# Adaptive modulation by matmuls, q and k projected by tokens, filter norms taken first

## The chip, the cores and the metric

The kernel runs on one core of a Trainium2 chip. The metric is the device time of one execution in microseconds, as the median of several runs. A core has five engines that run at the same time, each through its own list of instructions in order: TensorE (PE; matmuls, results go to PSUM; its weight loads are listed as PEld), VectorE (DVE), ScalarE (ACT), GpSimd (POOL) and SyncE (SP), which here issues nearly all DMAs. They wait for each other by semaphores.

## The reference

One layer of a diffusion backbone, for 2048 image tokens ("latent", cond vector `c`) and 256 text tokens ("prompt", cond vector `c_ctx`), width 1024:

```python
shift1, scale1, gate1, shift2, scale2, gate2 = split(silu(cond) @ w_mod + b_mod, 6)
u = (rms_norm(x, norm1_g) * (1 + scale1) + shift1) @ w_in
u_pool, u_hy, u_q, u_k, u_v = split(u)                  # 256, 768, 512, 512, 512 columns
y_hy = hyena_mixer(u_hy, ...)                           # two gated long convolutions by FFT
q = rms_norm(u_q.reshape(B, L, 8, 64), q_norm_g)        # per head of 64 channels
k = rms_norm(u_k.reshape(B, L, 8, 64), k_norm_g)
y = concatenate([pool_mixer(u_pool), y_hy, attend(q, k, u_v)]) @ w_out
x = x + gate1 * y
x = x + gate2 * (square(relu((rms_norm(x) * (1 + scale2) + shift2) @ w_up)) @ w_down)
```

The convolution filters are made in the kernel as well. `h` is a small network over positions, and for each of two directions and two orders

```python
k = (h @ f3_w).reshape(L, 2, 2, 256) * decay            # "taps"
filters = k / (sum(abs(k), over positions) + 1e-6)      # the filter's norm, one for a channel
```

## The kernel before

All data are float32. Precise products are made of three matmuls in a shorter format (`mm3`, lines 130 to 133): both operands are split into a high and a low half, and high x high, high x low and low x high are summed. A weight tile of 512 KB is loaded by `wtile` (line 123): the high half is made by ScalarE (line 117) or GpSimd (line 119), the low half `wl` by VectorE (line 120). There are three buffers for the raw tile and three for the halves. Other products (filters, modulation, transposes) are plain float32 matmuls, each of which the trace shows as two records.

Three generators issue the work, and `weave` (line 177) takes the next step from the one that lags most behind its share of declared costs: `dense` (line 1122), `latent_mixers` (line 999) and `prompt_mixers` (line 800). A planner then orders the instructions of each engine, with the order of issue as priority. `wait_for` holds a generator until a name is in `done`.

`dense` first computes shift1 and scale1 (`modulation_first`, line 221), then `u` in five runs of up to 512 tokens (line 1135; the fourth run is the prompt's 256 tokens), eight tiles of channels each. After each tile it takes `MODU[i]` steps of `modulation_rest` (line 326), which computes the other four sixths of the modulation: one load of 256 KB and the products for one block of 128 input channels a step, VectorE for one cond vector and ScalarE with GpSimd for the other. The partial sums `macc` have channels along the free dimension and are summed over partitions by matmuls with a column of ones (line 346).

Then `proj_qkv` (line 258) projects q, k and v, in runs of 512 tokens (and one of 256), in the order of `JOBS` (line 256). For q and k a tile of 128 channels (two heads) by all tokens of the run is made with the weight as stationary operand (matmuls of 512 columns). v is made by tokens: the tokens are the stationary operand and 256 channels the moving one; it holds two weight tiles, each of half of the input channels, until the job's end. The head norms of q and k need a sum over 64 channels, that is over partitions: the squares are split, and two matmuls with the block matrix `headsum` (line 265) spread the sums to all partitions. `rstd` (line 135) makes the inverse root by four steps of ScalarE and two of VectorE. This is done for a tile in `finish`, one job later.

`filters` (line 432) runs in the latent generator while `dense` makes `u`. For each order `o` (`filter_latent`, line 477) a first loop makes the 16 taps tiles (`filter_taps`, line 398: four matmuls of 64 rows by 256 columns, a product with the loaded decay, magnitudes by ScalarE, sums of them by GpSimd) and keeps all in 16 buffers; `filter_rinv` makes the inverse norms; a second loop scales each tile (`filter_finish`, GpSimd) and transforms it (`time_to_freq`). For `o = 1` the generator waits for `u` and `ln` between the two loops. The prompt's filters (`prompt_filters`) use the same functions.

`aux_tile` (line 217) gives the one PSUM bank that the dense stream uses besides its three accumulators. After `proj_qkv` come the output projections and the MLP, with the latent attention beside them.

Of the kernel before, what the change touches and what calls it, by code (L numbers as in the profile page):

```python
# [10 lines left out]
F32 = mybir.dt.float32  # L11
# [8 lines left out]
P = 128  # L20
# [7 lines left out]
DH = 64  # L28
# [27 lines left out]
def tile_hybrid_step(ctx: ExitStack, tc: tile.TileContext, a: dict):  # L56
# [33 lines left out]
    headsum = ctile([P, P], "headsum", F32R)  # L90
    for e in range(2):
        for f in range(2):
            nc.gpsimd.memset(headsum[64 * e:64 * e + 64, 64 * f:64 * f + 64].bitcast(F32), float(e == f))

# [40 lines left out]
    def rstd(pool, ss, n, shape):  # L135

        r = pool.tile(shape, F32, tag="rsr", name="r", bufs=1)
        v = xp.tile(shape, F32, tag="tmp", name="v")
        t = xp.tile(shape, F32, tag="tmp", name="t")
# [80 lines left out]

    def modulation_first(lp):
# [18 lines left out]
        pmt = acc_tile()  # L240
        mrow = xp.tile([P, 512], F32, tag="raw", name="mrow", bufs=3)
        nc.vector.tensor_copy(mrow, pm)
        for q in range(4):
            nc.tensor.transpose(pmt[:, q * P:(q + 1) * P], mrow[:, q * P:(q + 1) * P], ident)
        pmv = pmt.rearrange("p (q j r) -> p j q r", q=4, j=4)

        def halves(t):
            return t.rearrange("p (j q) -> p j q", j=2)

# [6 lines left out]
    JOBS = ((1, 0), (1, 1), (1, 2), (1, 3), (2, 0), (0, 0), (0, 1), (0, 2), (0, 3), (2, 1))  # L256

    def proj_qkv(qp, hT, T0, n):
# [3 lines left out]
        def finish(comp, j, raw, sq):  # L262
            pss = aux_tile()[:, :n]
            for i in range(2):
                nc.tensor.matmul(pss, headsum, sq[i], start=(i == 0), stop=(i == 1))
            r = rstd(qp, pss, DH, [P, n])
            nc.vector.scalar_tensor_tensor(out=raw, in0=raw, scalar=(qg8, pvs("kg"))[comp], in1=r, op0=ALU.mult, op1=ALU.mult)
            nc.sync.dma_start(out=(qT, kT)[comp][j][:, T0:T0 + n], in_=raw)
            if comp == 1 and T0 == NL:
                nc.sync.dma_start(out=a["new_kT"][j * P:(j + 1) * P, :], in_=raw)  # L270

        def rows(dst, r0, cs):
            return dst[r0:r0 + 2 * P, cs].rearrange("(e p) c -> p e c", p=P)

        for comp, part in JOBS:
            if comp == 2:
                W = [wtile("w_v", 2 * part + kk, 4, (None, nc.gpsimd)[kk]) for kk in range(2)]
                cs = slice(part * 256, (part + 1) * 256)
                for t in range(0, n, 2 * P):
                    pp = acc_tile()  # L280
                    for e in range(2):
                        ts = slice(t + e * P, t + (e + 1) * P)
                        for k in range(KD):
                            mm3(pp[:, e * 256:(e + 1) * 256], hT[k][0][:, ts], hT[k][1][:, ts], W[k // 4][0][:, k % 4, :], W[k // 4][1][:, k % 4, :], k == 0, k == KD - 1, skip_group_check=True)
                        yield 2600
                        while todo:
                            finish(*todo.pop(0))
                    v = qp.tile([P, 2, 256], F32, tag="q", name="v")
                    nc.scalar.activation(v.rearrange("p e c -> p (e c)"), pp, AF.Copy)
                    if T0 < NL:  # L290
                        nc.sync.dma_start(out=rows(vd, T0 + t, cs), in_=v)
                    else:
                        nc.sync.dma_start(out=rows(vpd, 0, cs), in_=v)
                        nc.sync.dma_start(out=rows(a["new_v"], 0, cs), in_=v)
                continue
# [4 lines left out]
            while todo:  # L300
                finish(*todo.pop(0))
# [1118 lines left out]
```

## Time and profile before

| | |
|---|---|
| median of 3 runs | 3247.18 us (3244.32 to 3251.28) |
| the profiled execution | 3239.31 us |
| its span (first to last instruction) | 3237.4 us |
| PE busy | 3008.9 us (93%) |
| DVE busy | 2104.9 us (65%) |
| ACT busy | 1507.1 us (47%) |
| POOL busy | 1179.4 us (36%) |
| mean granted TensorE clock | 0.959 |

The profile is of one execution. Shares over the whole span hide the stages, so the views are read by stretch. In the view by windows a row is one stretch: its bounds and length, then for PE, PEld, DVE, ACT and POOL the busy microseconds with the number of instructions, then the granted clock of TensorE as a share of 2.4 GHz, the busy share of the DMA engines and the GB/s that they moved. In the groups of instructions a row names the line, the engine, the operation, the tiles (out<-in), their shapes and the count; then the busy microseconds and the mean nanoseconds of one, and after the second bar the idle time of the engine just before them and what ended it. Matmuls are pipelined: a record is longer than the distance to the next start.

### The profile page before, as it was taken

Reading aid. Unit: us, or ns where it says so; the run is one execution under the profiler, and the core shown is the slowest. Engines: PE = TensorE matmul, PEld = TensorE weight load, DVE = VectorE, ACT = ScalarE, POOL = GpSimd, SP = SyncE. Lnnn points to the kernel's source line nnn. Section 1 sums busy time; section 2 is a strip of 40 time slices with the busy share of each in tenths; the row PEclk is TensorE's granted clock in tenths of the full one; section 3 lists DMA queues with packets and bytes.
Section 4 is the critical chain, followed back from the end, with each engine's and each line's share of the span. In section 5 each row is a group of like instructions: output and inputs, shape, how many; then the busy total and the mean of one; then the engine's idle time right before and its main releaser. Section 6 shows DMA issues by size and latency. Waiting matters only on the chain.

```text
span 3237.4 us, 44877 instructions
## 1 busy us (share of the span) xinstructions
PE 3008.9 (93%) x15997; PEld 2483.3 (77%) x15997; DVE 2104.9 (65%) x3090; ACT 1507.1 (47%) x2803; POOL 1179.4 (36%) x996
## 2 busy tenths in 40 slices
PE   4989888878898899999999999899999999999999
PEld 1777677766777898986887777688878888788887
DVE  8797967997857977787666555544463444644443
ACT  3556455554656656666555554322342223432222
POOL 3777745566424523445333332311131111311111
PEclk8999888888998999999999999999999999999999
DMA  6657476556855596553334324322324223232322
GB/s 220 190 161 250 140 231 218 188 189 195 274 173 190 163 313 196 180 186 107 123 114 126 111 94 154 115 96 98 124 85 150 98 93 122 91 118 97 98 98 85
DMA packets 252862, 489.99 MB, mean 151 GB/s; under 512 B 23508, under 2 KB 124569, under 8 KB 252316
## 3 DMA queue, kind: packets, MB, share of 16 engines
q1 hardware_dynamic: 245437, 464.83, 44.1%
q0 software_dynamic: 7200, 22.28, 2.4%
q8 instruction: 127, 2.08, 0.3%
q14 instruction: 98, 0.79, 0.1%
HBM read 417.67 MB, written 70.13 MB: 151 GB/s over the span
## 4 chain that ended last, share of the span: by engine, by line
PE 68%; DVE 15%; DMA 6%; issue 4%; POOL 4%; ACT 3%; SPq 1%; DVEq 0%; ACTq 0%; POOLq 0%
PE pm L131 19%; PE pm L132 19%; PE pm L133 19%; PE po L867 3%; PE ppt L846 2%; DVE wl L120 2%; PE ps L832 1%; PE ps L833 1%; DMA dc<-in_decay 1%; POOL kk L419 1%; DVE macc L338 1%; DMA wm<-in_w_mod 1%; DVE hl L171 1%; PE pf L131 1%; POOL ssq L155 1%
## 5 line engine op out<-in xcount | busy, mean ns | idle before, releaser
L131 PE MATMUL pm<-hh,wh 128*128 128x512 f32 (+1 forms) x2240 | 850.0, 382 | 37.8 <-ACT hh L117 17.6
L120 DVE TENSOR_TENSOR wl<-wraw,wh 128x1024 fp32r<-128x1024 f32 x460 | 608.0, 1323 | 424.7 <-ACT wh L117 403.6
L132 PE MATMUL pm<-hl,wh 128*128 128x512 f32 (+1 forms) x2240 | 847.6, 379 | 16.7 <-DVE hl L171 12.4
L133 PE MATMUL pm<-hh,wl 128*128 128x512 f32 (+1 forms) x2240 | 845.1, 378 | 6.7 <-DVE wl L120 6.7
L117 ACT ACTIVATE wh<-wraw 128x1024 fp32r<-128x1024 f32 x430 | 454.5, 1058 | 765.7 <-PE pm L132 673.5
L120 POOL TENSOR_TENSOR al<-r,ah 128x512 fp32r<-128x512 f32 (+1 forms) x160 | 200.8, 1256 | 975.2 <-ACT ah L117 975.0
L131 PEld LDWEIGHTS pm<-hh,wh 128*128 128x128 f32 x2240 | 435.0, 195 | 116.8 <-ACT hh L117 19.1
L132 PEld LDWEIGHTS pm<-hl,wh 128*128 128x128 f32 x2240 | 434.6, 194 | 95.8 <-DVE hl L171 14.8
L133 PEld LDWEIGHTS pm<-hh,wl 128*128 128x128 f32 x2240 | 433.8, 194 | 81.9 <-DVE wl L120 8.0
L133 PE MATMUL pm<-ah,wl 128*128 128x512 f32 (+1 forms) x1280 | 475.8, 372 | 0.1
L131 PE MATMUL pm<-ah,wh 128*128 128x512 f32 (+1 forms) x1280 | 471.9, 372 | 4.0 <-ACT ah L117 2.5
L132 PE MATMUL pm<-al,wh 128*128 128x512 f32 (+1 forms) x1280 | 474.1, 371 | 1.2 <-POOL al L120 1.2
L1094 DVE SCALAR_TENSOR_TENSOR x<-pm,gate,x 128x512 f32<-128x512 f32 (+1 forms) x320 | 221.1, 695 | 273.3 <-PE pm L133 272.5
L131 PEld LDWEIGHTS pm<-ah,wh 128*128 128x128 f32 x1280 | 240.4, 188 | 47.0 <-ACT ah L117 2.7
L132 PEld LDWEIGHTS pm<-al,wh 128*128 128x128 f32 x1280 | 241.4, 189 | 43.7 <-POOL al L120 1.4
L133 PEld LDWEIGHTS pm<-ah,wl 128*128 128x128 f32 x1280 | 241.4, 189 | 41.8 <-issue 0.8
L838 POOL TENSOR_SCALAR sS<-sS,rl 128x736 f32<-128x736 f32 (+5 forms) x128 | 117.7, 920 | 201.1 <-DVE rl L837 127.2
L969 POOL TENSOR_TENSOR Tt<-bias,mask 128x360 f32<-128x360 f32 (+5 forms) x96 | 102.4, 1067 | 180.1 <-DVE m L981 147.5
L117 ACT ACTIVATE ah<-r 128x512 fp32r<-128x512 f32 (+1 forms) x160 | 93.8, 588 | 151.4 <-DVE r L1077 150.9
L155 POOL TENSOR_TENSOR ssq<-ssq,sqr 128x512 f32<-128x512 f32 (+1 forms) x70 | 97.7, 1396 | 135.5 <-ACT sqr L154 135.5
L986 ACT ACTIVATE sS<-sS,m 128x480 f32<-128x480 f32 (+5 forms) x128 | 77.2, 603 | 112.0 <-DVE m L985 107.7
L1077 DVE TENSOR_TENSOR r<-r 128x512 f32<-128x512 f32 (+1 forms) x160 | 118.1, 739 | 1.5 <-ACT r L1076 1.3
(317 smaller groups left out, 5044.7 us busy)
## 6 DMA issues: line engine op xcount, KB each, us to landing
wraw<-in_w_up SPq DMA_DIRECT2D x160, 512.0 KB
wraw<-in_w_down SPq DMA_DIRECT2D x160, 512.0 KB
wraw<-in_w_u SPq DMA_DIRECT2D x40, 512.0 KB
dftw<-in_S POOLq DMA_DIRECT2D x40, 512.0 KB, 6.4
wraw<-in_w_qk SPq DMA_DIRECT2D x40, 512.0 KB
wraw<-in_w_out SPq DMA_DIRECT2D x40, 512.0 KB
x<-in_xT_sample SPq DMA_DIRECT2D x64, 256.0 KB
wm<-in_w_mod SPq DMA_DIRECT2D x64, 256.0 KB
```

The source lines that it names most:

```text
L117: nc.scalar.activation(hi, raw, AF.Copy)
L120: lo_eng.tensor_tensor(out=lo, in0=raw, in1=hi.bitcast(F32), op=ALU.subtract)
L131: nc.tensor.matmul(out, lh, rh, start=start, stop=False, **kw)
L132: nc.tensor.matmul(out, lh, rl, start=False, stop=False, **kw)
L133: nc.tensor.matmul(out, ll, rh, start=False, stop=stop, **kw)
L155: nc.gpsimd.tensor_tensor(out=acc, in0=acc, in1=sq, op=ALU.add)
L838: nc.gpsimd.tensor_scalar(out=sc_[:, :tot], in0=sc_[:, :tot], scalar1=r, scalar2=1.0, op0=ALU.mult, op1=ALU.mult)
L867: nc.tensor.matmul(po[64 * e:64 * e + 64, ocol:ocol + P], vap(e, n), pt[:n, col * P:(col + 1) * P], start=(q == 0), stop=(q == len(chunks) ...
L969: nc.gpsimd.tensor_tensor(out=t_, in0=bias[e][:, bro:bro + nr, bco:bco + ncol], in1=mask[rc * 3 + cc_], op=ALU.add)
L986: nc.scalar.activation(sS[:, :n], sS[:, :n], AF.Exp, bias=m4[:, 2:3], accum_out=m4[:, 3:4])
L1077: nc.vector.tensor_tensor(out=r, in0=r, in1=r, op=ALU.mult)
L1094: nc.vector.scalar_tensor_tensor(out=xs[j], in0=po, scalar=gate2[:, j, c:c + 1], in1=xs[j], op0=ALU.mult, op1=ALU.add)
```

## The change

There are four parts. `modulation_rest` now multiplies on TensorE: a step loads four tiles of 256 KB, runs one matmul for each with the two cond vectors (padded to 32 columns) as stationary operand, into four 32-row strips of one auxiliary PSUM bank, and adds that bank to `acc`. Two halves of eight steps make all four sixths; the result is turned by four transposes (`modulation_rows`, cut out of `modulation_first`). Steps are taken after every other tile of `u`.

q and k are projected by tokens like v, in six jobs in place of ten, from weights that are stored by 256 channels (`w_qkv`). The squares are summed by heads along the free dimension, the inverse root is made on 16 columns at most, and the result is turned back to channels by transposes.

The latent filters' norms are made ahead of both orders, from taps with channels as rows (`decayT` is the decay turned). The inverse norms are spread by matmuls and scale the last weight, `f3n`, so the taps come out normed and each is transformed as it is made. Taps and transforms share one loop, which for `o = 1` stands behind the wait for `u`.

`rstd` takes a `size` for the small tiles. The `headsum` constant goes.

```diff
-    JOBS = ((1, 0), (1, 1), (1, 2), (1, 3), (2, 0), (0, 0), (0, 1), (0, 2), (0, 3), (2, 1))
+    JOBS = ((1, 0), (1, 1), (2, 0), (0, 0), (0, 1), (2, 1))
...
+        def finish(comp, part, t, raw, r, out):
+            heads = raw.rearrange("p (e h d) -> p (e h) d", e=2, h=4)
+            nc.vector.tensor_tensor(out=heads, in0=heads, in1=r[:, t // 32:t // 32 + 8, None].to_broadcast([P, 8, DH]), op=ALU.mult)
+            tr = aux_tile()
+            for c in range(2):
+                for e in range(2):
+                    nc.tensor.transpose(tr[:, (2 * c + e) * P:(2 * c + e + 1) * P], raw[:, e * 256 + c * P:e * 256 + (c + 1) * P], ident)
+            nc.scalar.activation(out[:, :, t:t + 256], tr.rearrange("p (c t) -> p c t", c=2), AF.Copy, scale=(qg8, pvs("kg"))[comp])
...
         for comp, part in JOBS:
...
+            W = [wtile("w_qkv", 4 * comp + 2 * part + kk, 4, (None, nc.gpsimd)[kk]) for kk in range(2)]
...
+            for t in range(0, n, 2 * P):
+                pp = acc_tile()
+                for e in range(2):
+                    ts = slice(t + e * P, t + (e + 1) * P)
+                    for k in range(KD):
+                        mm3(pp[:, e * 256:(e + 1) * 256], hT[k][0][:, ts], hT[k][1][:, ts], W[k // 4][0][:, k % 4, :], W[k // 4][1][:, k % 4, :], k == 0, k == KD - 1, skip_group_check=True)
+                    if e == 0 and todo:
+                        finish(*todo.pop(0))
+                    yield 2600
+                v = qp.tile([P, 512], F32, tag="q", name="v", bufs=3)
+                nc.scalar.activation(v, pp, AF.Copy)
+                if comp < 2:
+                    sq = xp.tile([P, 512], F32, tag="tmp", name="sq")
+                    nc.scalar.activation(sq, v, AF.Square)
+                    nc.vector.tensor_reduce(out=ss[:, t // 32:t // 32 + 8], in_=sq.rearrange("p (h d) -> p h d", d=DH), axis=AX.X, op=ALU.add)
...
+                r = rstd(qp, ss, DH, [P, n // 32], "small")
...
     def modulation_rest(lp):
-        for ch in range(8):
...
+        for half in range(2):
+            acc = lp.tile([P, 512], F32, tag="macc", name="macc", bufs=1)
             for k in range(KD):
+                wm = []
+                for g in range(4):
+                    wm.append(lp.tile([P, 512], F32, tag="wm2", name="wm2", bufs=4))
+                    c0 = 2048 * (1 + half) + 512 * g
+                    nc.sync.dma_start(out=wm[g], in_=a["w_mod"][k * P:(k + 1) * P, c0:c0 + 512])
+                pb = aux_tile()
+                for g in range(4):
+                    nc.tensor.matmul(pb[32 * g:32 * g + 32, :], sc[:, k, :], wm[g], start=True, stop=True, skip_group_check=True)
...
+                    nc.vector.tensor_tensor(out=acc, in0=pb, in1=acc, op=ALU.add)
                 yield 600
...
+            with scope("norms") as fp:
+                sums = fp.tile([P, 8, 4], F32, tag="sums", name="sums", bufs=1)
+                for c in range(2):
+                    for b in range(4):
+                        for d in range(2):
+                            dt = fp.tile([P, 512], F32, tag="dt", name="dt", bufs=4)
+                            nc.sync.dma_start(out=dt, in_=a["decayT"][d, c * P:(c + 1) * P, b * 512:(b + 1) * 512])
+                            r = slice(d * 64, (d + 1) * 64)
+                            for o in range(2):
+                                pf = psum()
+                                nc.tensor.matmul(pf, f3[r, o * 256 + c * P:o * 256 + (c + 1) * P], h2[r, b * 512:(b + 1) * 512], start=True, stop=True)
+                                junk = fp.tile([P, 512], F32, tag="junk", name="junk")
+                                j = 4 * o + 2 * d + c
+                                nc.vector.tensor_tensor(out=junk, in0=pf, in1=dt, op=ALU.mult)
+                                nc.scalar.activation(junk, junk, AF.Abs, accum_out=sums[:, j, b:b + 1])
+                        yield 1700
...
             def filter_latent(o):
...
-                    for i in range(0, 16, 2):
-                        kks += filter_taps(fp, psum, f3, o, acc, lambda r, e: h2[r, i + e:NL:16], lambda d: a["decay"][d, :, i:i + 2, :], 16)
-                        yield 1000
-                    ri = filter_rinv(fp, psum, acc)
                     if o:
                         yield from wait_for("u", "ln")
                         zp = stack.enter_context(scope("p2u"))
                     for i in range(0, 16, 2):
+                        kf, kb = normed_taps(fp, psum, f3n, o, lambda r, e: h2[r, i + e:NL:16], lambda d: a["decay"][d, :, i:i + 2, :])
...
+                        yield 1000
                         w = dft_load(fp, "S1", i)
-                        kf, kb = kks[i:i + 2]
-                        filter_finish(fp, o, kf, 0, ri, i == 0)
-                        filter_finish(fp, o, kb, 1, ri, i == 0)
...
-    MODU, MODQ = (0, 1, 1, 1, 2), (0, 2, 2, 1, 1)
+    MODU, MODQ = (0, 1, 1, 1, 0), (0, 1, 1, 1, 1)
...
-                    for _ in range(MODU[i]):
+                    for _ in range(MODU[i] if step % 2 else 0):
                         next(mods, None)
```

## Rows read from the trace of the kernel before

**Rows 1.** The windows view: input stretch, q/k/v stretch, its start, the rest.

```profile
50.00:425.00 375.00, 310.92 (x1415) 248.26 (x1414) 320.28 (x390) 185.48 (x299) 266.06 (x184) 0.89 0.56 176
425.00:1050.00 625.00, 533.15 (x3031) 457.89 (x3030) 494.54 (x628) 355.95 (x678) 322.31 (x288) 0.91 0.65 208
425.00:525.00 100.00, 95.94 (x593) 84.88 (x592) 65.97 (x74) 63.04 (x113) 35.67 (x35) 0.99 0.76 245
1250.00:3237.40 1987.40, 1956.43 (x10062) 1597.59 (x10058) 1089.77 (x1765) 822.11 (x1580) 504.90 (x431) 0.99 0.36 116
```

**Rows 2.** TensorE's waits, 0 to 1250 us: total us, times, longest.

```profile
PE pm L132 <- DVE hl L171: 12.4, 5, 7.5
PE n L265 <- DVE sql L120: 12.3, 12, 1.9
```

**Rows 3.** SyncE's queue, 0 to 1250 us: a wait of its DMA issues.

```profile
SPq L333 <- POOL macc L340: 74.8, 33, 6.7
```

**Rows 4.** Groups of VectorE by form, 0 to 1250 us: modulation, then q and k.

```profile
L338 DVE SCALAR_TENSOR_TENSOR macc<-wm,sc,macc 128x512 f32<-128x512 f32 x56 | 54.6, 976 | 16.9 <-DMA wm<-in_w_mod 16.8
L144 DVE SCALAR_TENSOR_TENSOR t<-t,v 128x512 f32<-128x512 f32 x36 | 33.0, 918 | 27.0 <-ACT t L143 27.0
L120 DVE TENSOR_TENSOR sql<-sq,sqh 128x512 fp32r<-128x512 f32 x32 | 30.3, 946 | 15.7 <-POOL sqh L119 15.7
L267 DVE SCALAR_TENSOR_TENSOR q<-q,pv,r 128x512 f32<-128x512 f32 x16 | 17.3, 1080 | 0.4
```

**Rows 5.** Lines 338 and 411, 0 to 1250 us: shortest, median, longest ns.

```profile
L338 DVE SCALAR_TENSOR_TENSOR macc<-wm,sc,macc x56: 731/750/1786, 46.8 to 861.2; 128x512 f32<-128x512 f32 x56
...
L411 DVE TENSOR_TENSOR kk<-pf,dc x32: 673/678/692, 94.7 to 324.3; 128x512 f32<-128x512 f32 x32
```

**Rows 6.** The weight split's low half, first 50 to 425 us, then after 1250.

```profile
L120 DVE TENSOR_TENSOR wl<-wraw,wh 128x1024 fp32r<-128x1024 f32 x40 | 66.5, 1662 | 8.9 <-ACT wh L117 8.9
...
L120 DVE TENSOR_TENSOR wl<-wraw,wh 128x1024 fp32r<-128x1024 f32 x315 | 397.0, 1261 | 378.6 <-ACT wh L117 372.0
```

**Rows 7.** Groups of GpSimd by form, 0 to 1250 us.

```profile
L340 POOL TENSOR_TENSOR macc<-macc,wm 128x512 f32<-128x512 f32 x56 | 86.1, 1537 | 68.1 <-ACT wm L339 67.5
L419 POOL TENSOR_TENSOR kk<-kk,rinv 128x512 f32<-128x512 f32 x36 | 58.8, 1668 | 4.0 <-DVE rinv L395 4.0
L414 POOL TENSOR_TENSOR acc<-acc,ab 128x512 f32<-128x512 f32 x36 | 55.0, 1535 | 29.7 <-ACT ab L413 29.4
...
L119 POOL TENSOR_SCALAR sqh<-sq 128x512 fp32r<-128x512 f32 x32 | 25.9, 808 | 88.2 <-ACT sq L305 88.2
```

**Rows 8.** A step of the inverse root on ScalarE, 0 to 1250 us.

```profile
L140 ACT ACTIVATE r<-n,epsc 128x512 f32<-128x512 f32 x36 | 24.6, 684 | 10.3 <-PE n L265 10.2
```

**Rows 9.** TensorE's timeline: start, length; starts of both matmul forms.

```profile
499.87 0.39 PE L131 MATMUL pm<-hh,wh 128*128 128x512 f32 x1
500.09 0.39 PE L132 MATMUL pm<-hl,wh 128*128 128x512 f32 x1
...
505.18 0.28 PE L131 MATMUL pm<-wh,hh 128*128 128x256 f32 x1
505.30 0.27 PE L132 MATMUL pm<-wl,hh 128*128 128x256 f32 x1
```

**Rows 10.** The same timeline: strips, the start of taps, row sums, transposes.

```profile
31.78 1.06 PE L239 MATMUL pm<-wm,sc 128*32 128x512 f32 x8
...
90.45 0.39 PE L132 MATMUL pm<-hl,wh 128*128 128x512 f32 x1
90.77 1.26 PE L405 MATMUL pf<-f,h 64*128 64x256 f32 x8
...
895.15 1.62 PE L346 MATMUL n<-ones,macc 128*128 128x2 f32 x14
896.63 0.64 PE L902 MATMUL pb<-ident,sS 128*128 128x128 f32 x4
```

**Rows 11.** Matmuls of the v projection, whole span, the first of three groups.

```profile
L131 PE MATMUL pm<-wh,hh 128*128 128x256 f32 x288 | 82.0, 285 | 2.7 <-ACT q L303 2.7
```

More of the change, by code (lines that the diff above doesn't have):

```diff
@@ L219, in aux_tile, with modulation_rows, halves @@
         return aux[0].tile([P, 512], F32, tag="n", name="n") if aux else acc_tile()
+    def modulation_rows(pmt, rows):
+        mrow = xp.tile([P, 512], F32, tag="raw", name="mrow", bufs=3)
+        nc.vector.tensor_copy(mrow, rows)
+        for q in range(4):
+            nc.tensor.transpose(pmt[:, q * P:(q + 1) * P], mrow[:, q * P:(q + 1) * P], ident)
+        def halves(t):
+            return t.rearrange("p (j q) -> p j q", j=2)
+        return pmt.rearrange("p (q j r) -> p j q r", q=4, j=4), halves
     def modulation_first(lp):
@@ L239, in modulation_first @@
                     nc.tensor.matmul(pm[r:r + 32, :], sc[:, k, :], wm[:, j * 512:(j + 1) * 512], start=(k == 0), stop=(k == KD - 1), skip_group_check=True)
[L240 to L248, printed above, removed]
+        pmv, halves = modulation_rows(acc_tile(), pm)
         for c in range(2):
@@ new lines, in finish @@
+        def finish(comp, part, t, raw, r, out):
[6 more added lines that the diff above has]
+            nc.scalar.activation(out[:, :, t:t + 256], tr.rearrange("p (c t) -> p c t", c=2), AF.Copy, scale=(qg8, pvs("kg"))[comp])
+            if t + 256 < n:
+                return
+            for c in range(2):
+                j = 2 * part + c
+                nc.sync.dma_start(out=(qT, kT)[comp][j][:, T0:T0 + n], in_=out[:, c])
+                if comp == 1 and T0 == NL:
+                    nc.sync.dma_start(out=a["new_kT"][j * P:(j + 1) * P, :], in_=out[:, c])
@@ L334, in modulation_rest @@
                 if k == 0:
[L335 to L340 removed]
+                    nc.scalar.activation(acc, pb, AF.Copy)
+                else:
+                    nc.vector.tensor_tensor(out=acc, in0=pb, in1=acc, op=ALU.add)
@@ L341, in modulation_rest @@
                 yield 600
-            pb = aux_tile()
-            for c in range(2):
-                for j in range(4):
-                    q = 2 * (c * 4 + j)
-                    nc.tensor.matmul(pb[:, q:q + 2], acc[c][:, j * P:(j + 1) * P], ones[:, 0:2], start=(q == 0), stop=True, skip_group_check=True)
-            pbv = pb[:, 0:16].rearrange("p (c j e) -> p c j e", c=2, e=2)
-            dst, nm = ((gate1, "bm_g1"), (S2m, "bm_s2"), (G2, "bm_c2"), (gate2, "bm_g2"))[kind]
-            for c in range(2):
-                nc.vector.tensor_tensor(out=dst[:, half * 4:half * 4 + 4, c], in0=pbv[:, c, :, 0], in1=pvs(nm, half * 4, 4), op=ALU.add)
+            pmv, halves = modulation_rows(aux_tile(), acc)
@@ L351, in modulation_rest @@
+            for j, (dst, nm) in enumerate((((gate1, "bm_g1"), (S2m, "bm_s2")), ((G2, "bm_c2"), (gate2, "bm_g2")))[half]):
+                for c in range(2):
+                    nc.vector.tensor_tensor(out=halves(dst[:, :, c]), in0=pmv[:, 2 * j:2 * j + 2, :, c], in1=halves(pvs(nm, 0, 8)), op=ALU.add)
             yield 1000
```

124 lines of the change are left out of this document (58 added, 66 removed).

## The prediction

> **What bounds the kernel now.** I read the windows view by stretch first, then the waits of TensorE, then the groups of instructions engine by engine. The windows [rows 1] split the program in two. After 1250 us TensorE is busy 1956 of 1987 us at a granted clock of 0.99: there it is the limit, and nothing of the change lies there. Before that it is not. In the input stretch (50 to 425 us) it is idle 64 of 375 us and the clock is 0.89, so 22% of the stretch, 82 us, runs on the lower of the two levels (1.2 instead of 2.4 GHz); in the q, k, v stretch (425 to 1050 us) it is idle 92 of 625 us, and 18%, 112 us, runs on the lower level. Time on the lower level loses at most half of itself, 97 us in both. So there is a pool of some 156 + 97 = 253 us that a better supplied TensorE could take back. VectorE is busy 85% and 79% in these stretches, GpSimd 71% and 52%. The row of 425 to 525 us shows the other condition: VectorE at 66%, and TensorE busy 95.9 of 100 us at clock 0.99. TensorE's waits [rows 2] end on many vector results (the low half of the normed input, the low half of the squares), none of them long: a queueing loss, not one chain. SyncE's queue also stands 74.8 us behind GpSimd's modulation sums [rows 3], with all later loads behind it.
>
> **The change part by part.**
>
> **VectorE.** The modulation's 64 products of two tokens go: 64 x 0.976 = 62 us [rows 4]. In their place come 14 sums of a PSUM tile into `acc` and two copies, 16 x 0.68 (the PSUM product `kk`, median 0.678 [rows 5]) = 11. q and k lose, for each of 36 full widths (32 tiles of 512 tokens and 8 of 256), the low half of the square (0.946), two steps of the inverse root (0.918 each) and the scaling (1.080) [rows 4]: 36 x 3.86 = 139. They gain 36 sums over heads (0.68, as the PSUM product) and 36 products with a broadcast (0.95, as the low half): 59; and 40 steps of the inverse root on 16 columns, between nothing and 0.9 each; the overhead of an instruction must remain, so I take 0.4, 16 in sum. The norms add 32 products from PSUM, 22, and small steps, 3; the two wide inverses that go are left out of the sum. Net: 62 - 11 + 139 - 75 - 25 = 90 us less.
>
> **GpSimd** loses the modulation's sums (56 x 1.537 = 86), the latent filters' 32 sums of magnitudes (1.535) and 32 scalings (1.668), and 36 widths of the high half of the squares (0.808) [rows 7]: 86 + 49 + 53 + 29 = 217 us of the 588 that it is busy in the two stretches, 37%, and gains nothing. This comes back on VectorE too: the modulation product, with two operands in SBUF, took 0.731 at least, 0.750 in the median and 1.786 at most, while the product that reads PSUM never left 0.673 to 0.692 [rows 5]. The unchanged weight split took 1.662 in the input stretch, where GpSimd is 71% busy, and 1.261 after 1250 us, where it is 25% busy [rows 6]. As an estimate: a quarter of the some 600 us of remaining two-operand work is such stretching, and 37% of that, some 50 us, goes.
>
> **ScalarE** loses 64 scaled copies and four steps for each of 36 inverse roots; at 0.684 [rows 8] that is 44 + 98. It gains 36 evacuations of transposes (25), 80 steps on 16 columns (at most 0.684, I take 0.3: 24), and the reads of 32 accumulators, short of 0.684 each, I take 6 in sum. Net 142 - 55 = 87 us less.
>
> **TensorE** gets more work. q and k turn from 512-column to 256-column matmuls with as many columns: starts lie 0.22 to 0.23 apart in the one form and 0.12 in the other [rows 9]. Before: 32 x 24 x 0.227 + 8 x 24 x 0.12 = 197; after: 36 x 48 x 0.12 = 207; plus 10. The `headsum` matmuls go (64 x 0.227 + 16 x 0.12 = 17). 144 transposes come; four took 0.64 with the tail of the last [rows 10], so 0.12 to 0.16 each: plus 17 to 23. The modulation's row sums leave (128 records at 1.62/14 = 0.116: 15), and 16 groups of four 32-row strips come, each group 8 records, 1.06 us [rows 10]: 17, plus 8 transposes, 1: plus 3. The norms add 32 matmuls of 64 rows by 512 columns. The nearest row is the taps': 8 records, four matmuls of 256 columns in two row halves, in 1.26 us [rows 10], 0.3 each, so 0.6 for 512 columns if the halves overlap and 1.2 if not: 19 to 38, I take 26, because two in a row share a half. The eight small norm products and the eight sums that go cancel. Sum: 10 - 17 + 17 + 3 + 26 = 39 us, bounds 30 to 58.
>
> One rule speaks against this. Before the taps' first start lies 0.32 us, against 0.23 elsewhere [rows 9, 10]: 0.09 for a change of the array's shape. The Trainium skill (TensorEngine Tiling (Array Packing), Key Properties) says that a change of tiling mode drains the engine. The 16 strip groups and up to 32 norm matmuls would make up to 96 such changes; at 0.09 this is 9 us, which by this rule would go on top.
>
> **Moved.** The taps of the second latent filter (32 of the 64 tap matmuls, 16 decay loads of 256 KB) move behind the wait for `u`, from the input stretch to just after 425 us, where each is woven with its transform. The modulation moves earlier: by lines 1100 and 326, 44 of its 64 loads stand in the input stretch instead of 36, and the other 20 beside the q, k, v of the prompt's 256 tokens, where 11 stood. So up to 16 + 9 loads, 6.5 MB, more fall right after 425 us, where DMA runs at 245 GB/s and a share of 0.76 [rows 1], that is 322 GB/s at full share: room in 100 us for 7.7 MB. It costs nothing if spread, 20 us (6.5 MB at 322 GB/s) if all of it must be waited for; I take nothing, as TensorE is busy 96% in that row. The norms' 4 MB of decay fall in the input stretch at a share of 0.56: covered. The modulation loads' buffers are now freed by matmuls, not by GpSimd, so SyncE's 74.8 us [rows 3] goes; behind a late load now stands TensorE itself, with four loads (1 MB, 3.3 us at full share) for 48 matmuls of a u tile pair, 11 us: covered.
>
> **Waits added.** A q, k job needs two weight tiles of three buffers until its end. The v jobs had this shape already, and TensorE idled 2.7 us before their 288 matmuls [rows 11]: nothing. The transposes of a job's last half wait for copy, square, sum, six small steps and product, some 0.68 each for the first three, 2 and 0.95, together 5 us, behind 24 matmuls of the next half, 2.9 us, and what the other streams place between. On TensorE everything stands behind a waiting transpose. Bounds: nothing, if the planner fills it as it does for the v jobs, to 2 us for each of 20 jobs, 40 us. I take nothing beyond the losses that the pool already holds, for the squares' waits (12.3 us at their low half [rows 2]) disappear.
>
> **The sum.** If the thousand microseconds ran like 425 to 525 us (4 us idle and half a microsecond of clock per 100), 253 us of loss would fall to 45: 208 back. VectorE falls from 815 to 815 - 90 - 50 = 675 busy us in 1000, near that row's 66%. I take half of the 208, 104, since many waits are latencies and loads that stay, less the 39 of added work: 65 us. The profiled execution took 3239.3 us (its span is 3237.4), so 3174; it lies 7.9 below the median of three, 3247.2, so **3182** as a median.
>
> **The rivals.**
> - *More comes back* (nearly all of the 208): 3247 - 208 + 39 = 3078. The row of 425 to 525 us speaks for it; that such a row stands alone among stretches with as many dependent steps speaks against. Between 3078 and 3140: 0.14.
> - *New waits take half of it*: the wait of the q, k transposes (40) or the loads after 425 us (20): 3202 to 3222, both together 3242. For it: vector results that end waits already [rows 2]. 0.19, of which 0.05 within 0.2% of before.
> - *TensorE was the bound already*: it is busy 83% and 85% of the two stretches, and its idle time ends on results whose latency, not throughput, counts. Then the added matmuls stand on the path and little returns: 3247 + 39 = 3286, at worst 3305. The point from which it decides is a return under 39 us, 15% of the pool. Against it: VectorE at 85% with such waits. 0.13.
> - *The transposes cost the clock.* After 1250 us the attention turns its scores by matmuls and the clock is 0.99 [rows 1], which speaks against it. Where each of 36 groups left the lower level on until the 24 matmuls behind it are over, it would cost 36 x 2.9 = 104: 3286. The Trainium skill (TensorE: Matmul & The Clock Gate, Part 4: PE-mode transpose) says that transposes do not count as busy for the clock; by that rule the chance were larger than the 0.02 that the row leaves.
> - *The changed order does nothing to the time* (the two effects cancel): 3247, 0.02.
>
> **How the numbers follow.** Forecast, 3140 to 3204 around 3182: 0.50. With the rivals: faster by over 0.2% (about what a measurement here can tell from no change; 6.5 us) 0.50 + 0.14 + 0.14 = 0.78; within 0.07; slower 0.15. The range from 3095 to 3255 leaves out some 0.05 below and 0.14 above.
>
> **What would show it.** Right: in the changed profile VectorE below 70% and GpSimd below 45% between 50 and 1000 us, the weight split near 1.3 us, the clock above 0.94 there, TensorE's whole busy time higher, and the last stretch (TensorE full) starting some 65 us earlier but as long. Wrong: transposes of q, k among TensorE's longest waits; the norm matmuls above 1.2 us; the DMA share at its limit after the input stretch; or idle time that stays although VectorE is free, which would mean that latencies and order, not throughput, made it.

## The result and the profile after

The changed kernel takes 3198.5 us (3194.9 to 3205.2) against 3249.2 for the kernel before beside it: 0.985 [0.982, 0.987], some 50 us faster, where 65 were forecast. Its profiled execution took 3199.6 us. First the page of the changed kernel (busy time, share, instructions of each engine):

```profile
span 3197.7 us, 46181 instructions
PE 3044.0 (95%) x16901; PEld 2512.5 (79%) x16901; DVE 1939.3 (61%) x3017; ACT 1427.5 (45%) x2721; POOL 958.1 (30%) x832
```

Against the table of before VectorE has 166 us less, GpSimd 221 less, ScalarE 80 less, and TensorE 35 more. TensorE's idle time falls from 228.5 (3237.4 - 3008.9) to 153.7 us. Where it fell shows in the windows of the changed kernel (the columns of [rows 1], whose stretches the first four are; the last is new):

```profile
50.00:425.00 375.00, 354.10 (x1668) 252.84 (x1667) 265.71 (x398) 181.39 (x321) 126.03 (x98) 0.95 0.63 202
425.00:1050.00 625.00, 565.74 (x4042) 520.60 (x4040) 445.85 (x636) 321.76 (x639) 251.66 (x233) 0.94 0.68 218
425.00:525.00 100.00, 99.28 (x710) 91.81 (x711) 61.16 (x82) 48.42 (x94) 26.86 (x24) 1.00 0.68 229
1250.00:3197.70 1947.70, 1915.12 (x9649) 1563.04 (x9647) 1048.83 (x1634) 779.37 (x1445) 493.41 (x401) 0.99 0.36 115
940.00:1030.00 90.00, 71.60 (x364) 55.91 (x364) 67.95 (x109) 52.02 (x111) 37.00 (x30) 0.77 0.44 133
```

In the input stretch TensorE is idle 21 us instead of 64 and the clock is 0.95 instead of 0.89. In the q, k, v stretch it is idle 59 instead of 92, at 0.94 instead of 0.91. The end is as full as before. But the last row is a hole that [rows 1] did not have: 940 to 1030 us, idle 18 of 90 at a clock of 0.77. What is missing there shows in the windows of the matmuls into `pm` alone, the tiles of the dense stream (same columns; first the changed kernel, then the kernel before):

```profile
948.00:1026.00 78.00, 0.00 (x0) 0.00 (x0) 0.00 (x0) 0.00 (x0) 0.74 0.36 110
```
```profile
948.00:1026.00 78.00, 61.21 (x307) 50.13 (x305) 0.00 (x0) 5.94 (x10) 0.96 0.56 188
```

For 78 us the dense stream runs no matmul. It has finished q, k and v (938 us) and what needs no attention of the prompt's output projection (947 us); next in it stands the rest of that projection (`head` at line 1230, behind `wait_for("prompt")`). What it waits for is the prompt's attention; its value matmuls in the instructions of one line (shortest, median, longest ns; first and last start), changed kernel and kernel before:

```profile
L957 PE MATMUL pbo<-ptS,pvt x32: 379/533/689, 939.1 to 1022.4; 128*64 128x256 f32 x32
```
```profile
L906 PE MATMUL pbo<-ptS,pvt x32: 379/379/431, 848.9 to 967.4; 128*64 128x256 f32 x32
```

Before, q, k and v ended at 1034 us, after the prompt's last step (967); now they end at 938, 96 us earlier, and the prompt's ends at 1022, 55 us later. What this wait costs the window can't say, for the mixers go on in it: TensorE as a whole is busy 71.6 of its 90 us. Two runs below bear on it.

The smaller signs: VectorE's groups between 0 and 1250 us (the weight split of [rows 6], then three new operations), ScalarE's new small steps, and SyncE's wait of [rows 3], in the changed kernel:

```profile
L115 DVE TENSOR_TENSOR wl<-wraw,wh 128x1024 fp32r<-128x1024 f32 x150 | 198.8, 1329 | 82.5 <-ACT wh L112 47.5 <-POOL wh L114 30.8 <-POOL pE L818 1.9
L267 DVE TENSOR_TENSOR v<-v,r 128x512 f32<-128x512 f32 x36 | 26.1, 761 | 0.5
L303 DVE TENSOR_REDUCE ss<-sq 128x8 f32<-128x512 f32 x36 | 24.4, 679 | 21.7 <-ACT sq L302 21.5
L514 DVE TENSOR_TENSOR junk<-pf,dt 128x512 f32<-128x512 f32 x32 | 21.7, 685 | 26.5 <-PE pf L511 18.4 <-issue 6.3 <-ACT junk L515 0.8
...
L515 ACT ACTIVATION_READ_ACCUMULATOR junk<-junk 128x1 f32 x32 | 6.0, 188 | 0.0
L135 ACT ACTIVATE r<-ss,epsc 128x16 f32<-128x16 f32 x16 | 4.9, 305 | 17.0 <-DVE ss L303 17.0
...
SPq L343 <- PE n L346: 26.7, 12, 5.1
```

### The profile page after: what moved, and what is told of

It is laid out like the page before. It is cut to its first block, busy times and chain, and to the rows that moved or that the text cites. A ratio compares the mean times of both kernels' runs of the same rounds, so it can differ in the third digit from the quotient of the medians.

```text
span 3197.7 us, 46181 instructions
## 1 busy us (share of the span) xinstructions
PE 3044.0 (95%) x16901; PEld 2512.5 (79%) x16901; DVE 1939.3 (61%) x3017; ACT 1427.5 (45%) x2721; POOL 958.1 (30%) x832
## 4 chain that ended last, share of the span: by engine, by line
PE 62%; DVE 2%; DMA 1%; ACT 1%; POOL 1%; issue 1%; SPq 0%; DVEq 0%; ACTq 0%; POOLq 0%
PE pm L126 18%; PE pm L128 18%; PE pm L127 18%; PE po L918 3%; PE ppt L897 2%; PE ps L883 1%; PE ps L884 1%; DVE xn L164 0%; DVE xn L169 0%; DVE wl L115 0%; DMA yraw<-yT 0%; DMA kin<-kT 0%; SPq L1009 0%; POOL ssq L150 0%; PE pm L154 0%
## 5 line engine op out<-in xcount | busy, mean ns | idle before, releaser
L126 PE MATMUL pm<-hh,wh 128*128 128x512 f32 (+1 forms) x1920 | 719.8, 377 | 19.6 <-ACT hh L112 11.4
L127 PE MATMUL pm<-hl,wh 128*128 128x512 f32 (+1 forms) x1920 | 718.2, 375 | 3.1 <-DVE hl L166 3.1
L128 PE MATMUL pm<-hh,wl 128*128 128x512 f32 (+1 forms) x1920 | 717.4, 374 | 0.0
L127 PEld LDWEIGHTS pm<-hl,wh 128*128 128x128 f32 x1920 | 365.7, 190 | 74.5 <-issue 10.0
L128 PEld LDWEIGHTS pm<-hh,wl 128*128 128x128 f32 x1920 | 365.4, 190 | 70.0 <-issue 9.0
L127 PE MATMUL pm<-wl,hh 128*128 128x256 f32 x864 | 249.5, 291 | 5.3 <-DVE wl L115 5.3
L126 PE MATMUL pm<-wh,hh 128*128 128x256 f32 x864 | 247.6, 291 | 5.7 <-ACT hh L112 4.6
L128 PE MATMUL pm<-wh,hl 128*128 128x256 f32 x864 | 247.4, 291 | 3.9 <-POOL hl L115 3.1
L127 PEld LDWEIGHTS pm<-wl,hh 128*128 128x128 f32 x864 | 167.2, 194 | 10.4 <-DVE wl L115 6.6
L126 PEld LDWEIGHTS pm<-wh,hh 128*128 128x128 f32 x864 | 166.5, 194 | 10.9 <-ACT hh L112 7.0
```

The lines of the kernel that those rows point to most:

```text
L126: nc.tensor.matmul(out, lh, rh, start=start, stop=False, **kw)
L127: nc.tensor.matmul(out, lh, rl, start=False, stop=False, **kw)
L128: nc.tensor.matmul(out, ll, rh, start=False, stop=stop, **kw)
```

## The experiments

All are compared with the kernel before in the same set of runs (3247.6 to 3251.1 us there). The first three put one part of the change alone into the kernel before.

**Modulation alone** (`modulation_rest` and `MODU`, `MODQ` of the diff).

```diff
+                    nc.tensor.matmul(pb[32 * g:32 * g + 32, :], sc[:, k, :], wm[g], start=True, stop=True, skip_group_check=True)
```

> The kernel before with the modulation part of the change alone (matmuls in four strips, steps of four loads). Theory (free vector engines let TensorE run): VectorE loses some 50 us, GpSimd 86, ScalarE 44, TensorE gains 3 to 9 us of work; GpSimd falls from 588 to about 500 busy us between 50 and 1050 us and the time falls by 15 to 40 us. Rival (TensorE was the bound already): no fall, 0 to 9 us slower. Rival (what counted was the load queue behind the GpSimd sums): nearly the whole gain of the change, 40 us or more, comes from this part alone.

Measured: 3230.0, 0.994 [0.992, 0.996], 18 us, within the theory's 15 to 40; the rival of the load queue (40 or more) did not come. In the input stretch TensorE's busy time rises from 311 to 321 and VectorE's falls from 320 to 271.

**q and k by tokens alone** (`proj_qkv`, `JOBS`, `rstd`).

```diff
-    JOBS = ((1, 0), (1, 1), (1, 2), (1, 3), (2, 0), (0, 0), (0, 1), (0, 2), (0, 3), (2, 1))
+    JOBS = ((1, 0), (1, 1), (2, 0), (0, 0), (0, 1), (2, 1))
```

> The kernel before with the q, k part alone (by tokens, norms by sums over the free dimension, transposes). Theory: VectorE loses some 64 us, GpSimd 29, ScalarE 50, all between 425 and 1050 us; TensorE's work changes by +10 - 17 + 13 = about +6 us; time falls by 15 to 40 us. Rival (the new chain in front of the transposes costs what the norms save): transposes among TensorE's longest waits and a time within 6 us of before. Rival (TensorE bound already): 6 us slower.

Measured: 3221.6, 0.992 [0.990, 0.995], 26 us, within the theory's range too. Nothing changes before 425 us; between 425 and 1050 TensorE's busy time is 555 instead of 533 at a clock of 0.94.

**Filter norms alone** (`norms`, `normed_taps` and the joined loop).

```diff
+            with scope("norms") as fp:
...
+                        kf, kb = normed_taps(fp, psum, f3n, o, lambda r, e: h2[r, i + e:NL:16], lambda d: a["decay"][d, :, i:i + 2, :])
```

> The kernel before with the filter part alone (norms first, taps normed by the last weight). It adds 26 to 35 us of TensorE work and 22 us of VectorE work and takes 102 us from GpSimd. Theory: GpSimd's relief shortens VectorE's two-operand work (weight split of the input stretch from 1.66 to about 1.45 us), which pays for most of the added matmuls: between 10 us faster and 20 us slower. Rival (TensorE bound already): 35 us slower. Rival (GpSimd was the real limit of the input stretch): 25 us or more faster.

Measured: 3282.4, 1.010 [1.008, 1.013]: 35 us slower, outside the theory's range and just what the rival said (TensorE bound already). TensorE's busy time is up by 42 us (3051.3).

**Norm matmuls side by side** in the changed kernel: for each order the two directions, which lie in the two halves of the rows, are issued one behind the other.

```diff
-                            for o in range(2):
-                                pf = psum()
+                        for o in range(2):
+                            pfs = [psum() for d in range(2)]
+                            for d in range(2):
```

> The changed kernel with the norm matmuls of the two directions issued side by side, so that the two row halves of the array can overlap. The trace of the changed kernel has each of the 32 at 1.06 us from its start to the next. Theory (after the change TensorE is the bound of the input stretch, busy 94%): if the halves overlap, a pair takes 1.2 us instead of 2.1, TensorE's work falls by 14 us and the time by 8 to 14 us. Rival (a pair must wait until both PSUM banks are empty): TensorE waits on the products there, and the time is the same or up to 10 us more.

Measured: 3196.9, 0.984 [0.981, 0.987], the same as the changed kernel. The timeline (start, length; a group of equal records in a row is one line) says why, in this kernel:

```profile
111.09 1.12 PE L513 MATMUL pf<-h,f 64*128 64x512 f32 x2
112.15 0.50 PE L126 MATMUL pm<-hh,wh 128*128 128x512 f32 x1
...
113.74 1.12 PE L513 MATMUL pf<-h,f 64*128 64x512 f32 x2
114.79 0.66 PE L597 MATMUL n<-ident,cy 128*128 128x128 f32 x4
```

Each matmul (two records) still stands alone; the planner puts dense matmuls between. The edit didn't bring the halves together, so whether they would overlap stays open. The busy time fell by 11 us, but the norms' own 64 records took 37.8 us against 37.6. The clock was 0.974 against 0.970, some 26 us less on the lower level, which as an estimate can make up to 13 us of busy time.

**Both gains without the filter part**: the changed kernel with `filters` of before.

```diff
-                        kf, kb = normed_taps(fp, psum, f3n, o, lambda r, e: h2[r, i + e:NL:16], lambda d: a["decay"][d, :, i:i + 2, :])
+                        kf, kb = kks[i:i + 2]
+                        filter_finish(fp, o, kf, 0, ri, i == 0)
+                        filter_finish(fp, o, kb, 1, ri, i == 0)
```

> The changed kernel with the filter norms put back as before, so modulation by matmuls and q, k by tokens together. Alone these two brought -18 and -26 us and the filter part cost +35, which adds up to -9 where the whole change brings -49. Theory A, the two gains add up and the filter part repays itself once the other two are there (it takes VectorE and GpSimd work out of the stretch): -44 us, about 3204, and so the filter part is worth -5 in their presence; TensorE busy about 3012. Theory B, the two other parts help each other and the filter part costs its 35 us everywhere: about 3163, faster than the changed kernel by 35. Theory C, the first two overlap in what they give back: -30, about 3218.

Measured: 3186.2, 0.982 [0.980, 0.983]: between A and B. The two parts together bring 61 us, more than 18 + 26, and the filter part costs 12 where they are present. Its page against that of the changed kernel:

```profile
PE 3004.3 (94%) x16837; PEld 2499.3 (78%) x16837; DVE 1938.0 (61%) x2986; ACT 1421.0 (45%) x2689; POOL 1045.7 (33%) x896
```

The filter part adds 40 us to TensorE and takes 88 from GpSimd, but nothing from VectorE (1938.0 and 1939.3). TensorE's idle time (3184.5 - 3004.3 = 180.2) falls by 26 with it: 40 paid, 26 returned.

**Another order of the bands**: the prompt's run last in `u` and first in q, k, v.

```diff
-    UORD, QORD = (0, 1, 2, 4, 3), (3, 4, 0, 1, 2)
+    UORD, QORD = (0, 1, 2, 3, 4), (4, 3, 0, 1, 2)
...
+            tp = hy.tile([P, NCH], F32, tag="tp", name="tp", bufs=1)
...
+            yp = hy.tile([P, 256], F32, tag="yp", name="yp", bufs=1)
```

> The changed kernel with the bands taken in another order: the prompt band is last of u and first of q, k and v, so that its q, k and v are ready some 40 us earlier, and two small tiles of the prompt's mixers have one buffer instead of two. In the changed kernel q, k, v end at 938 us and the dense stream then waits for the prompt's mixers until 1023 us, with TensorE busy 182 of 220 us between 940 and 1160 at a clock of 0.77 to 0.90. Theory A, that wait gives back part of the gain: the prompt's mixers end nearer to q, k, v, the wait shrinks by 30 to 60 us, and the time falls by 15 to 40 us, to 3160 to 3185. Theory B, the prompt's mixers are held up by their own chain and by the filters, not by q, k and v: no change, 3190 to 3206.

Measured: 3180.4, 0.979 [0.978, 0.981], 18 us below the changed kernel. The prompt's attention now ends 130 us earlier, and the dense stream has matmuls in the hole (first the line of the attention, then the windows of `pm` alone):

```profile
L957 PE MATMUL pbo<-ptS,pvt x32: 379/379/690, 787.8 to 893.1; 128*64 128x256 f32 x32
...
948.00:1026.00 78.00, 36.05 (x251) 33.29 (x250) 7.48 (x16) 1.99 (x5) 0.85 0.55 178
```

So the time is in the range of A. That the 18 us are the price of the wait is not shown by this run: TensorE's idle time fell by 5 us only (153.7 to 148.4). The rest is busy time, as less time on the lower level can make it (0.030 x 2 x 3198 = 192 us there in the changed kernel, 0.023 x 2 x 3178 = 146 here; at most half of the difference, 23 us).

**Spare work on GpSimd** in the changed kernel.

```diff
+                nc.gpsimd.tensor_tensor(out=bal, in0=bal, in1=bal, op=ALU.add)
...
+                    ballast(2)
...
+                    ballast(1)
```

> The changed kernel with GpSimd work added that nobody waits for: 188 additions of a 128 by 512 tile to itself, two in each step of u and one in each of q, k, v, some 190 us, near the 210 us that the change took from GpSimd there (and two small tiles of the prompt's mixers have one buffer instead of two). Theory A, the gain came through VectorE, whose instructions are stretched less when GpSimd is idle (86 of its 103 us of saved time between 50 and 1050): VectorE's time there rises from 712 to 770 to 800 us and the kernel loses 30 to 80 us, to 3230 to 3280. Theory B, the gain came from shorter chains, steps that no longer stand in front of a release of TensorE, and spare work on GpSimd costs little: 3195 to 3215.

**Spare work on VectorE**, issued in the same places, one each.

```diff
+                nc.vector.tensor_reduce(out=bals, in_=bal.rearrange("p (h d) -> p h d", d=DH), axis=AX.X, op=ALU.add)
```

> The changed kernel with VectorE work added that nobody waits for: 148 reductions of a 128 by 512 tile, one in each step of u and of q, k, v, some 100 us, as much as the change took from VectorE between 50 and 1050 (and two small tiles of the prompt's mixers have one buffer instead of two). Theory A, VectorE's time in that stretch is what holds TensorE: VectorE's time there rises from 712 to about 815 us and the kernel loses 40 to 80 us, to 3240 to 3280. Theory B, the shorter chains count and not VectorE's load: 3195 to 3215.

Measured: 3234.8, 0.996 [0.995, 0.998], with GpSimd's, 36 us above the changed kernel; 3225.8, 0.994 [0.993, 0.996], with VectorE's, 27 above. The groups: the spare work and the weight split of 50 to 425 us with GpSimd's, the same split in the changed kernel, and VectorE's spare work:

```profile
L1183 POOL TENSOR_TENSOR bal<-bal 128x512 f32<-128x512 f32 x188 | 234.1, 1245 | 9.4 <-DVE bal L1179 0.3
L115 DVE TENSOR_TENSOR wl<-wraw,wh 128x1024 fp32r<-128x1024 f32 x40 | 65.5, 1637 | 22.1 <-ACT wh L112 17.5 <-PE n L346 3.5 <-PE pm L128 0.7
```
```profile
L115 DVE TENSOR_TENSOR wl<-wraw,wh 128x1024 fp32r<-128x1024 f32 x42 | 57.0, 1358 | 19.3 <-ACT wh L112 17.3 <-PE n L346 1.7
```
```profile
L1183 DVE TENSOR_REDUCE bals<-bal 128x8 f32<-128x512 f32 x148 | 100.0, 676 | 0.9
```

Nobody waits for the spare work, and it did not run spread over both stretches, but early. The windows of its tile alone show where (busy VectorE and GpSimd in the first, VectorE in the second):

```profile
50.00:425.00 375.00, 0.00 (x0) 182.03 (x145) 0.92 0.57 183
425.00:1050.00 625.00, 0.00 (x0) 27.94 (x23) 0.95 0.69 221
```
```profile
0.00:50.00 50.00, 18.92 (x28) 0.86 0.88 319
50.00:425.00 375.00, 81.12 (x120) 0.95 0.60 190
```

So both runs say something of the input stretch, and next to nothing of the q, k, v stretch. It costs 36 us for 234 us of GpSimd (0.15 each), 27 for 100 of VectorE (0.27 each); the first is in the range of A, the second lies between A and B. The load of both engines holds TensorE there, but only by a part of itself. (As in the run before, two small tiles have one buffer; that was not tried alone.) The way from GpSimd is the one that was expected: with its spare work the split goes back to 1.637 us (1.662 in [rows 6]), and the 3017 VectorE instructions that both kernels have took 55 us more in sum (worked out from the traces). Between 50 and 1050 VectorE's time rises only from 712 to 731, but with 990 instructions in that window instead of 1034. At 0.27 the 55 us would cost 15 of the 36, as an estimate. The rest may be GpSimd's own steps of the normed input, which stand behind the spare work in its queue; that was not separated.

**The order and the old norms together**: the two diffs above.

```diff
-    UORD, QORD = (0, 1, 2, 4, 3), (3, 4, 0, 1, 2)
+    UORD, QORD = (0, 1, 2, 3, 4), (4, 3, 0, 1, 2)
...
+                        filter_finish(fp, o, kf, 0, ri, i == 0)
```

> The two changes that helped, together: filter norms as in the kernel before (that gave 3186 with the changed kernel's other parts) and the prompt band last in u and first in q, k, v (that gave 3180 with all parts). Theory A, both gave back the same thing, the dense stream's wait for the prompt's mixers (85 us long in the changed kernel, 9 us between the end of q, k, v and that of the prompt's attention with the norms as before): together they bring no more than one of them, 3175 to 3190. Theory B, the norms' matmuls cost TensorE's time wherever they stand (some 35 us of records, of which 12 us came out with the norms as before), and the order's gain is another: the two add up, 3160 to 3172.

Measured: 3159.6, 0.973 [0.972, 0.974]. They more than add up (B): this is the fastest of all, 39 us below the changed kernel where the two alone brought 12 and 18, and the filter part costs 21 us here. It also bears on the wait. With the old norms alone (the run that gave 3186) the prompt's attention ends at 994 us and the dense stream hardly pauses, as the rows of that run show (the attention, then the windows of `pm` alone):

```profile
L911 PE MATMUL pbo<-ptS,pvt x32: 379/379/430, 882.8 to 994.4; 128*64 128x256 f32 x32
...
948.00:1026.00 78.00, 49.95 (x365) 46.75 (x365) 6.49 (x14) 2.35 (x4) 0.96 0.56 182
```

There the other order brought 27 us (3186.2 to 3159.6), more than the 18 where the hole is. So the order helps in another way than by ending this wait, and what the hole cost stays open.

**The order and the norms side by side.**

```diff
-    UORD, QORD = (0, 1, 2, 4, 3), (3, 4, 0, 1, 2)
+    UORD, QORD = (0, 1, 2, 3, 4), (4, 3, 0, 1, 2)
...
+                            pfs = [psum() for d in range(2)]
```

> The changed kernel with the prompt band last in u and first in q, k, v, and with the norm matmuls of the two directions (the two halves of TensorE's rows) side by side. Side by side alone took 11 us of TensorE's busy time and 2 us of the time (less than the measurement resolves), with the wait for the prompt's mixers still there. Theory A, that wait hid the gain of TensorE's 11 us, and without it they show: 3165 to 3174. Theory B, in that stretch TensorE's time is not what is short and they stay hidden: 3176 to 3184.

Measured: 3182.9, 0.980 [0.979, 0.982], no change. Its expectation took the 11 us of busy time for a saving of the norms; as said above they were the clock's, and here the 32 matmuls stand alone again (37.8 us for 64 records). It decides nothing.

**A quarter of the norms** in the changed kernel: it leaves out three quarters of the positions that each norm sums over.

```diff
-                        for d in range(2):
+                        for d in range(2 if b == 0 else 0):
...
-                nc.vector.tensor_reduce(out=ri, in_=sums, axis=AX.X, op=ALU.add)
+                nc.vector.tensor_copy(ri, sums[:, :, 0])
```

> The changed kernel with the filters' norms summed over the first quarter of the taps alone: 24 of the 32 norm products by matmul are left out, with their loads, products and magnitudes (48 records of 0.59 us, 28 us of TensorE; 16 us of VectorE), while the steps that the planner counts stay, so that the taps start as late as before. Theory A, the filter part costs because TensorE has 37 us more to do there: 16 to 28 us less, 3170 to 3182, at or below the kernel with the old norms (3186). Theory B, it costs because the filters' chain starts later (taps at 204 us, 81 with the old norms) and TensorE's time is not short: 3190 to 3200.

**A later start with the old norms.**

```diff
             f3 = f3_tile(kp)
+            for _ in range(8):
+                yield 1700
+            yield 1000
```

> Modulation by matmuls and q, k by tokens with the norms as in the kernel before (3186), but the filters' stream is held by the planner for as many counted steps as the norms would take (8 of 1700 and one of 1000) before its taps; no instruction is added. Theory A, a later start of the filters costs nothing in itself: 3180 to 3192. Theory B, the later start is what the filter part costs: 3196 to 3215.

Measured: a quarter of the norms 3181.3, 0.978 [0.977, 0.980], 17 us below the changed kernel; the later start 3177.8, 0.977 [0.976, 0.979], not slower than 3186. Both go with A (the second lies 2 us below its range). With the later start the planner began the taps at 81 us all the same, so their start was not moved; but the filters' chain ended later (the last inverse transform at 1126 us, 1094 with the old norms alone and 1100 in the changed kernel), and that cost nothing. With a quarter of the norms TensorE's busy time fell by 41 us, but the taps also started earlier (118 instead of 205 us), so that run moved two things. A late end of the chain is thus not what is paid; a late start of the taps by itself was not tested. That the filter part costs because TensorE has more to do is the reading that fits all of these runs.

## Why the prediction was right, step by step

**The bound** was read rightly: before 1250 us TensorE was short of supply, and in the input stretch both runs with spare work show that VectorE's and GpSimd's load is a part of what it pays for. For the q, k, v stretch only the 26 us of q and k alone speak. The clock rose with the supply (0.89 to 0.95, 0.91 to 0.94); the last stretch stayed as it was.

**The engines' sums.** GpSimd -221 (forecast -217), ScalarE -80 (-87). VectorE -166 (-140): the stretching was sized rightly. The 2820 instructions that both kernels have in the same number took 53 us less in sum (worked out form by form from the traces), where 50 was taken; the 86 us that the expectation of the spare GpSimd work names is not found this way. The undervalued term was the work that comes and goes: 122 us less in sum of records, not 90, with q's and k's old steps at 149 (139 taken), the products with a broadcast at 0.76 (0.95 taken) and some 10 us of old inverses that the sum had left out. The sums over heads and the products from PSUM took 0.68, as taken from [rows 5]. VectorE's share between 50 and 1050 fell to 71%, not below 70, since work moved in from later.

**TensorE's sum** was 39 and should have been near 49. The rows of the changed kernel behind this (groups between 0 and 1250 us, then the timeline):

```profile
L511 PE MATMUL pf<-h,f 64*128 64x512 f32 x64 | 37.6, 668 | 4.9 <-DVE fx L484 4.9
L346 PE MATMUL n<-wm,sc 128*32 128x512 f32 x128 | 25.3, 613 | 1.8 <-ACT qo L272 1.1 <-ACT plt L596 0.6
...
111.56 0.39 PE L127 MATMUL pm<-hl,wh 128*128 128x512 f32 x1
111.87 1.12 PE L511 MATMUL pf<-h,f 64*128 64x512 f32 x2
112.93 0.50 PE L128 MATMUL pm<-hh,wl 128*128 128x512 f32 x1
113.26 0.39 PE L126 MATMUL pm<-hh,wh 128*128 128x512 f32 x1
...
430.78 0.60 PE L271 MATMUL n<-ident,v 128*128 128x128 f32 x4
431.13 0.36 PE L128 MATMUL pm<-wh,hl 128*128 128x256 f32 x1
```

- The norms: one matmul takes 1.06 us (111.87 to 112.93), 34 in all, not 26. "Because two in a row share a half" failed: no two stand in a row. The bound of 19 to 38 held.
- The strips: 25.3 us busy against the 17.4 of the row sums that left, and 1 for transposes: +9, not +3. The shape was read at full speed from [rows 10], and its mean here is 1.6 a step.
- The transposes of q, k: 36 x 0.35 (430.78 to 431.13) = 13, not 17. Neither the rival of their waits nor that of their clock came: ScalarE's copy of them is the only thing that held TensorE, by 0.2 us, and the stretch from 425 to 525 runs at 1.00.
- Changes of the array's shape: the starts are 0.31 apart before a norm and 0.33 behind the first matmul after it, against 0.23; some 0.09 each. By the Trainium skill (TensorEngine Tiling (Array Packing), Key Properties) a change of tiling mode drains the engine, and the trace agrees so far (0.31 and 0.33 us against 0.23). At 0.09 the 96 changes would add 9 us to the 49.

**What came back.** 50 gained and 49 of work mean that some 99 us came back, 108 with the changes of shape (89 and 98 between the two profiled executions, which are 40 apart); the step "half of the 208, 104" was right in size. The half was a choice that no row gave, and the sum knew neither the loss of the filter part nor the order of the streams: that it came out so close is in part luck. The two can be seen apart: 75 us less idle, and at most half of the 73 us less on the lower level (0.041 x 2 x 3237 = 265 against 0.030 x 2 x 3198 = 192), 37. As an estimate, at the prices of the spare work (0.27 for each of VectorE's 166 us; for GpSimd's 221 the 0.09 that are left when VectorE's 15 of the 36 are taken out) some 65 of the 99 are accounted for; the rest was not separated. Of the 15 us between forecast and result 10 are the mis-sized terms of TensorE's sum, seen in the rows above, and the rest is within what the estimate can hold.

**What was missed.** First, which stream runs ahead: q, k and v overtook the prompt's mixers, and a step that was hidden became a wait. The prediction asked what is late next only for the new steps, not for the one line at the end of the stretch where the dense stream waits for another. With the other order of the bands the same change gives 18 us more; but the hole is there only when all three parts stand together (with the old norms there is next to none), and without it the order gives 27, so the price of the wait itself is not known. Second, the three parts were summed into one. Taken apart, GpSimd's 88 us of the filter part were worth less than TensorE's 40: at the price of its spare work 88 x 0.15 = 13, and 26 by TensorE's idle time. The rival "TensorE was the bound already" was right of this part where it stands alone (35 us paid for 42 of busy time); beside the other two it cost 12 of 40, and 21 of some 48 in the new order. Why it costs more alone was not settled. The latent attention's first scores start 70 us later with it where it stands alone (1294.8 against 1224.6 us), 65 later in the new order (1177.7 against 1112.9) and 2 in the changed kernel (1130.5 against 1128.7), which goes with its price, but no run tests this. Nor was it settled why modulation and q, k together bring more (61) than their sum (44).

**Moved.** DMA ran at a share of 0.68 right after 425 us with TensorE busy 99.28 of 100: the moved loads cost nothing, as taken. SyncE's wait, which was taken to go, fell from 74.8 to 26.7 us and is now one for TensorE's strips.

## What to carry to other kernels

Price a change part by part, each with what it adds to the fullest engine and what it takes from the others; the 40 us that the filter part adds to TensorE cost 12 to 35, while a microsecond of a neighbour's load was worth 0.15 to 0.27 in the input stretch. When a stretch gets shorter, look at the wait at its end, and try what it waits for first: here that was worth as much as a part of the change, though not by the wait alone, as the same edit in a kernel without the wait showed. Spare work that nobody waits for is a price for an engine's load only in the stretch where it really ran. And an edit that puts two instructions side by side in the program doesn't always do so on the engine where a planner weaves other streams in between.

## What the runs showed of the hardware

VectorE's operations with both operands in SBUF lose time beside GpSimd: in the input stretch the split of a weight went from 1.358 to 1.637 us under spare GpSimd work, near the 1.662 of [rows 6], while VectorE's sums over heads and its products from PSUM stayed at 0.68. GpSimd's spare addition itself took 1.245 us where VectorE's products of that size took 0.73 at the shortest ([rows 5]). A plain float32 matmul of 64 rows by 512 columns that stands alone held TensorE for 1.06 us, nearly as long as four of 256 columns together in both halves of the rows (1.26, [rows 10]).
